# A four-layer mixer in f32r on one core: order of weight loads, of the first stores, and of the last tiles of an out-projection

## The chip, the core and the metric

The kernel runs on one core of one Trainium2 chip. Its time is the device time of one execution in microseconds (us); lower is better. Engines are named as in the profile: PE is TensorE's matmuls (PEld its weight loads), DVE is VectorE, ACT is ScalarE, POOL is GpSimd, SP is SyncE, which here issues nearly all DMAs from one queue that runs in order.

## The reference, cut to what matters

The input x has 2048 rows (tokens) of 1024 values in float32. Four layers follow each other. Each has one projection in, a mixer of its own, one projection out, a residual and (except the last) a layer norm:

```python
def reference(x, ...):
    x = first_block(x, ...)      # layer 1
    x = second_block(x, ...)     # layers 2 and 3
    return third_block(x, ...)   # layer 4

# the frame of every layer
h = jnp.einsum('btd,de->bte', x, w_in)        # 1024 -> 2560 to 4360 columns
mix = mixer(h)                                 # see below, 1024 columns
out = jnp.einsum('bte,ed->btd', mix, w_out)    # 1024 -> 1024
z = ALPHA * x + out                            # layer 4: x + out, and no norm behind it
x = (z - mu) * lax.rsqrt(var + LN_EPS) * ln_g + ln_b
```

The mixers are: layer 1, a gated linear recurrence in chunks and sliding-window attention with sinks; layer 2, gated linear attention and a spatial gating unit; layer 3, retention and multi-scale pooling; layer 4, banded attention, an mLSTM and a gated convolution, with an RMS norm of the input ahead. None of the mixers is touched by the change.

## The kernel before

**Blocks.** The 2048 tokens are four blocks of 512, each of four tiles of 128. `run` (the end of the class) goes through the blocks in pairs: layer 1 on blocks 0 and 1, layer 2 on blocks 0 and 1, layers 3 and 4 likewise, then all four layers on blocks 2 and 3. That makes sixteen pairs of layer and block.

**Split operands.** A float32 product is made of three f32r matmuls: each operand is split into a rounded part (`hi`, for the input `ah`) and the rest (`lo`, `al`), and hi x hi, hi x lo and lo x hi are added up in PSUM.

**Weights.** Weights come in pieces of 128 x 1024 (some 128 x 528 or 128 x 544), by `weight` (L441). The first time that a piece is used (layer and block 0) it is loaded unsplit into a staging tile `wst` (two buffers), cast by ACT into `hi` (L450), and DVE subtracts to get `lo` (L315, the helper of every two-tensor operation). The split piece, tile `whl` (four buffers, 1 MB each), is then stored to DRAM (tile `wdr`, L454). In the other three blocks the piece is ready: one DMA brings it back (L446). A projection in has 20 to 36 pieces, a projection out eight. The first projection of a block, `in_b4`, holds four pieces at a time and does the first 256 tokens with each of them, then the other 256: eight groups of 24 matmuls.

**Who sets the order.** Every instruction is written once in program order; a scheduler then sets each engine's fixed order at build time, by priority and by its own estimate of times. `hp()` makes what is written inside it count as 2500 instructions earlier, `later(n)` as n instructions later; `keep_in_program_order` keeps the marked instructions in the order in which they are written. `weight` is all inside `hp()`, and at the start (`self.start`) its loads and those of the input are kept in program order by `first`.

**The start.** `load_x` (L521 and on) loads the first block's input in eight tiles of 256 KB (tile `u`, L545), two at a time, each two followed by one of the first four weight pieces. ACT casts the input into `ah` (L548), DVE subtracts into `al` (L315).

**The projection out** (`out_proj`). The output has two halves of 512 columns. The first half takes four pieces, and for each the four tiles of tokens in turn, in four PSUM banks (`acc`). The second half takes pieces 4 to 7 all at once and goes tile by tile: all eight chunks of tile 0, then tile 1, and so on, 24 matmuls a tile, and behind each tile its residual (L312), statistics (L628), the reciprocal root by nine small DVE operations (`rstd1`: tiles `ve`, `vy`, `vh`, `vf`, `vt`) and the norm. Even tiles are normed by ACT (`nm`, `vy`) without gain and bias; odd ones by four DVE operations. What is left of a tile (`tail`: eight transposes on PE, `mm<-ident,big`, their copies and stores, and for even tiles four POOL operations on the tile) is put off, and `flush` writes it between the groups of the next block's `in_b4`. Layer 4 has no norm and no tail: its tiles are stored (`out_dram`, L625).

Of the kernel before, what the change touches and what calls it, by code (L numbers as in the profile page):

```python
# [10 lines left out]
F32 = mybir.dt.float32  # L11
# [5 lines left out]
ALU = mybir.AluOpType  # L17
# [209 lines left out]
class Build:  # L227
    def __init__(self, ctx, tc, I, O, layers=(1, 2, 3, 4), nblk=NB):
        self.tc, self.nc, self.I, self.O = tc, tc.nc, I, O
        self.layers, self.nblk = layers, nblk  # L230
        pool = lambda name, bufs, **k: ctx.enter_context(tc.tile_pool(name=name, bufs=bufs, **k))
        self.c1 = pool("c1", 1)
        self.wst = pool("wst", 2)
        self.whl = pool("whl", 4)
        self.up = pool("up", 13)
        self.tp = pool("tp", 7)
        self.sp = pool("sp", 4)
        self.lp = pool("lp", 1)
        self.bp = pool("bp", 1)
        self.dp = pool("dp", 1, space=bass.MemoryType.DRAM)  # L240
        self.wdr = pool("wdr", 1, space=bass.MemoryType.DRAM)
        self.parts = {}
        self.ps_a = pool("ps_a", 4, space=PSUM)
        self.ps_m = pool("ps_m", 4, space=PSUM)

# [193 lines left out]
    def weight(self, name, i, n=1024):  # L439
        nc = self.nc  # L440
        with self.hp():  # L441
            w = self.whl.tile([128, 2, n], F32R, tag="whl", name="whl")
            hi, lo = w[:, 0], w[:, 1]
            kept = self.parts.get((name, i))
            if kept is not None:
                nc.sync.dma_start(w.bitcast(F32), kept)  # L446
                return hi, lo
            st = self.wst.tile([128, n], F32, tag="wst", name="wst")
            self.first(nc.sync.dma_start(st, self.I[name][i][:, 0:n]))
            nc.scalar.copy(hi, st)  # L450
            self.tt(lo, st, hi.bitcast(F32), ALU.subtract)
            if self.nblk > 1:
                kept = self.wdr.tile([128, 2, n], F32, tag=f"{name}_{i}", name="wdr")
                nc.sync.dma_start(kept, w.bitcast(F32))  # L454
                self.parts[name, i] = kept
        return hi, lo

    def next_w(self, n=1024):
        if self.ahead:
# [61 lines left out]
    def load_x(self, b, l):  # L521
        if not self.start:
            for t in range(4):
                for i in range(2):
                    self.load_x1(b, l, t, i)
            return

        ws = []
        self.wi, self.wpos = "wi1", 0
        for parts in (((0, 0), (1, 0)), ((0, 1), (1, 1)), ((2, 0), (3, 0)), ((2, 1), (3, 1))):  # L530
            for t, i in parts:
                with self.hp():
                    self.load_x1(b, l, t, i)
            ws.append(self.next_w())
        self.ahead, self.start = ws, False

    def first(self, ins):
        if self.start:
# [36 lines left out]
    def out_proj(self, layer, b, split):  # L575
# [35 lines left out]
        for j in range(4):  # L611
            hi, lo = self.weight(wo, 4 + j)
            ws.append((hi.rearrange("p (k c) -> p k c", k=2), lo.rearrange("p (k c) -> p k c", k=2)))
            if j == 0:
                for i in range(2):
                    for t in range(0):
                        self.out_mm(acc[t], t, i, ws[0][0][:, i], ws[0][1][:, i])
        for t in range(4):
            for k in range(2 if t < 0 else 0, 8):
                hi, lo = ws[k // 2]  # L620
                self.out_mm(acc[t], t, k, hi[:, k % 2], lo[:, k % 2])
            x = self.xr[:, t, 512:1024]
            self.stt(x, x, alpha, acc[t], ALU.mult, ALU.add)
            if layer == 4:
                nc.sync.dma_start(self.O[b * TB + t * 128:b * TB + t * 128 + 128, :], self.xr[:, t])  # L625
                continue
            st = sts[t]
            nc.vector.bn_stats(st[:, 6:12], x)  # L628
            x = self.xr[:, t]
            mv = self.s(2, "mv")  # L630
            nc.vector.bn_aggr(mv, st)
            y = self.rstd1(mv[:, 1:2], 1.0, 1e-5)
            if not last and t % 2 == 0:
                nm = self.s(1, "nm")
                self.stt(nm, mv[:, 0:1], -1.0, y, ALU.mult, ALU.mult)
                self.act(x, x, AF.Identity, scale=y, bias=nm)
                continue
            for i in range(2):
                xi = x[:, i * 512:i * 512 + 512]
                self.stt(xi, xi, mv[:, 0:1], lng[i], ALU.subtract, ALU.mult)  # L640
                self.stt(xi, xi, y, lnb[i], ALU.mult, ALU.add)
            if last:
                nc.sync.dma_start(self.O[b * TB + t * 128:b * TB + t * 128 + 128, :], x)
# [1111 lines left out]
    def run(self):  # L1755
        self.setup()

        self.todo = [(l, c) for b in range(0, self.nblk, 2) for l in self.layers for c in range(b, b + 2)]
        self.lc = None
        while self.todo:  # L1760
            l, c = self.todo.pop(0)
            self.load_x(c, l)
# [36 lines left out]
```

## Time and profile before

| | |
|---|---|
| median of three runs | 3770.92 us (3770.17 to 3778.2) |
| the profiled execution's own time | 3774.09 us |
| its span, first to last instruction | 3772.3 us |
| PE busy | 3677.3 us (97%) |
| DVE, ACT, POOL busy | 2177.9, 1384.2, 542.1 us |
| DMA | 798.04 MB, 212 GB/s over the span |
| mean granted clock of PE | 0.995 |

Busy times are shares of the span; PE's matmuls are pipelined and their ends are modelled, so that a busy PE need not be a PE at its peak. A wait is put down to what ended it. The granted clock is the share of full speed that the throttle left to PE.

### The profile page before, as it was taken

The numbers are of one execution on the slowest core, as the hardware profiler recorded it, in microseconds if no ns is written. First come the engines' busy times: TensorE is split into PE (matmuls) and PEld (weight loads), VectorE is DVE, ScalarE is ACT, GpSimd is POOL, SyncE is SP. The second block draws the span as 40 slices with busy tenths as digits, with TensorE's granted clock in tenths as the row PEclk, the third lists the DMA queues.
The fourth block names the chain that finished last, engine by engine and source line by source line (L and its number), as shares of the span: only waits on it lengthen the run. The fifth ranks groups of instructions, "written<-read, shape, count | busy, mean of one in ns | idle before, by whom it ended". The sixth has DMA issues, their size and how long they took to land.

```text
span 3772.3 us, 53592 instructions
## 1 busy us (share of the span) xinstructions
PE 3677.3 (97%) x20576; PEld 3100.4 (82%) x20576; DVE 2177.9 (58%) x5387; ACT 1384.2 (37%) x2889; POOL 542.1 (14%) x445
## 2 busy tenths in 40 slices
PE   7999999999999999999999999999999999999999
PEld 6788888887888888788888878888887878888887
DVE  6765556555655598577456455443544545872873
ACT  5636343323241354325254263312221313441441
POOL 0020111112121200300200201111121311011002
PEclk9999999999999999999999999999999999999999
DMA  6775567855886576752544645747565756435434
GB/s 229 261 263 177 187 239 273 311 199 195 300 304 215 213 260 223 261 197 101 208 179 164 226 152 187 255 161 256 185 231 206 253 193 246 146 140 209 177 123 157
DMA packets 161680, 798.04 MB, mean 212 GB/s; under 512 B 17936, under 2 KB 18064, under 8 KB 93840
## 3 DMA queue, kind: packets, MB, share of 16 engines
q1 hardware_dynamic: 161424, 794.62, 58.4%
q8 instruction: 162, 2.65, 0.3%
q14 instruction: 94, 0.77, 0.1%
HBM read 593.02 MB, written 201.52 MB: 211 GB/s over the span
## 4 chain that ended last, share of the span: by engine, by line
PE 49%; DVE 6%; DMA 2%; ACT 2%; issue 1%; POOL 0%; SPq 0%; DVEq 0%; POOLq 0%; ACTq 0%
PE acc L324 41%; PE mm L324 6%; PE mm L327 3%; DVE u L312 2%; DMA whl<-wdr 1%; DVE t L315 1%; ACT t L301 0%; DVE big L312 0%; DMA wst<-in_wo_dram 0%; DVE t L1034 0%; DVE ss L1400 0%; ACT u L301 0%; POOL mix L315 0%; DVE mix L312 0%; ACT u L1424 0%
## 5 line engine op out<-in xcount | busy, mean ns | idle before, releaser
L324 PE MATMUL acc<-whl,ah 128*128 128x512 f32 (+3 forms) x6144 | 1816.2, 380 | 15.1 <-DVE whl L315 4.1
L324 PEld LDWEIGHTS acc<-whl,ah 128*128 128x128 f32 x6144 | 1112.0, 188 | 242.9 <-issue 7.1
L324 PE MATMUL acc<-whl,al 128*128 128x512 f32 (+3 forms) x3072 | 1156.8, 377 | 0.0
L324 PE MATMUL acc<-ah,whl 128*128 128x256 f32 (+1 forms) x4096 | 1076.8, 346 | 46.0 <-DVE whl L315 17.3
L324 PEld LDWEIGHTS acc<-ah,whl 128*128 128x128 f32 x4096 | 707.1, 191 | 135.0 <-DVE whl L315 18.6
L324 PE MATMUL acc<-al,whl 128*128 128x512 f32 (+1 forms) x2048 | 699.2, 342 | 0.5 <-DVE al L315 0.2
L324 PEld LDWEIGHTS acc<-whl,al 128*128 128x128 f32 x3072 | 578.0, 188 | 114.0
L324 PEld LDWEIGHTS acc<-al,whl 128*128 128x128 f32 x2048 | 391.5, 191 | 40.5 <-issue 2.9
L315 DVE TENSOR_TENSOR whl<-wst,whl 128x1024 fp32r<-128x1024 f32 (+2 forms) x140 | 173.3, 1244 | 142.0 <-ACT whl L450 131.5
L315 POOL TENSOR_TENSOR big<-big,u 128x512 f32<-128x512 f32 x96 | 139.1, 1471 | 562.0 <-PE mm L327 421.6
L450 ACT CAST whl<-wst 128x1024 fp32r<-128x1024 f32 (+2 forms) x140 | 143.3, 1027 | 149.3 <-DMA wst<-in_wi_dram 76.1
L548 ACT CAST ah<-u 128x512 fp32r<-128x512 f32 x128 | 79.3, 619 | 307.0 <-PE acc L324 200.1
L312 DVE SCALAR_TENSOR_TENSOR g<-g,acc 128x512 f32<-128x512 f32 x80 | 54.6, 686 | 204.3 <-ACT g L301 204.2
L312 DVE SCALAR_TENSOR_TENSOR u<-mix,hdw,u 128x512 f32<-128x512 f32 x240 | 165.6, 742 | 0.1
L315 POOL TENSOR_TENSOR mix<-mix,g 128x512 f32<-128x512 f32 x56 | 77.4, 1385 | 592.2 <-DVE g L312 574.2
L312 DVE SCALAR_TENSOR_TENSOR big<-big,acc 128x512 f32<-128x512 f32 x128 | 86.7, 684 | 120.2 <-PE acc L324 118.5
L301 ACT ACTIVATE g<-acc 128x512 f32<-128x512 f32 x72 | 42.6, 596 | 232.0 <-PE acc L324 226.4
L301 ACT ACTIVATE t<-mm,cols 128x128 f32<-128x128 f32 (+2 forms) x272 | 99.6, 463 | 66.6 <-PE mm L327 62.7
L315 POOL TENSOR_TENSOR u<-u,lc 128x512 f32<-128x512 f32 (+1 forms) x64 | 68.0, 1070 | 326.1 <-issue 170.0
L315 DVE TENSOR_TENSOR al<-u,ah 128x512 fp32r<-128x512 f32 x128 | 89.7, 702 | 42.1 <-ACT ah L548 41.0
L324 PE MATMUL mm<-big,u 128*128 128x256 f32 (+2 forms) x616 | 94.3, 289 | 7.3 <-ACT big L923 1.8
L324 PEld LDWEIGHTS mm<-big,u 128*128 128x128 f32 x616 | 84.3, 191 | 16.0 <-ACT u L1424 3.2
(342 smaller groups left out, 4376.8 us busy)
## 6 DMA issues: line engine op xcount, KB each, us to landing
whl<-wdr SPq DMA_DIRECT2D x396, 1024.0 KB, 4.8
wdr<-whl SPq DMA_DIRECT2D x132, 1024.0 KB, 5.3
wst<-in_wi_dram SPq DMA_DIRECT2D x100, 512.0 KB, 6.9
rows<-big SPq DMA_DIRECT2D x48, 512.0 KB, 4.0
chn<-t SPq DMA_DIRECT2D x96, 256.0 KB, 6.3
u<-chn SPq DMA_DIRECT2D x96, 256.0 KB, 6.6
big<-rows SPq DMA_DIRECT2D x48, 512.0 KB, 7.1
wst<-in_wo_dram SPq DMA_DIRECT2D x32, 512.0 KB, 6.0
```

What stands on the lines that cost most here:

```text
L301: return self.nc.scalar.activation(out, in_, f, bias=bias, scale=scale)
L312: return self.nc.vector.scalar_tensor_tensor(out, in0, s, in1, op0, op1)
L315: return (eng or self.nc.vector).tensor_tensor(out, a, b, op)
L324: return self.nc.tensor.matmul(out, lhsT, rhs, start=start, stop=stop)
L327: return self.nc.tensor.transpose(out, in_, self.ident)
L450: nc.scalar.copy(hi, st)
L548: nc.scalar.copy(h, c4(st))
```

## The change

Three things change. (1) `weight` knows the order of all pieces (`pieces`), and when it is asked for a ready piece and one of the next two in that order is unsplit, it first writes that piece's load into `wst` (`stage`), ahead of the ready piece's load. (2) At the start, the very first piece is loaded, cast and subtracted in two halves; the four first pieces' stores are collected in `unsaved` and written behind all input loads and the layer's constants (`lc`), with a lower priority. (3) In the second half of a projection out, tiles 0 and 1 are accumulated together, chunk by chunk, and then tiles 2 and 3. Lines that did nothing before (`range(0)`, `t < 0`) go.

```diff
@@ -239,7 +239,7 @@
         self.bp = pool("bp", 1)
         self.dp = pool("dp", 1, space=bass.MemoryType.DRAM)
         self.wdr = pool("wdr", 1, space=bass.MemoryType.DRAM)
-        self.parts = {}
+        self.parts, self.staged, self.unsaved = {}, {}, []
         self.ps_a = pool("ps_a", 4, space=PSUM)
         self.ps_m = pool("ps_m", 4, space=PSUM)
 
@@ -441,19 +441,55 @@
         with self.hp():
             w = self.whl.tile([128, 2, n], F32R, tag="whl", name="whl")
             hi, lo = w[:, 0], w[:, 1]
+
+            assert self.order.pop(0) == (name, i, n)
+            if not self.start:
+                for a, k, m in self.order[0:2]:
+                    if (a, k) not in self.parts and (a, k) not in self.staged and (name, i) in self.parts:
+                        self.staged[a, k] = self.stage(a, k, m)
             kept = self.parts.get((name, i))
             if kept is not None:
                 nc.sync.dma_start(w.bitcast(F32), kept)
                 return hi, lo
-            st = self.wst.tile([128, n], F32, tag="wst", name="wst")
-            self.first(nc.sync.dma_start(st, self.I[name][i][:, 0:n]))
-            nc.scalar.copy(hi, st)
-            self.tt(lo, st, hi.bitcast(F32), ALU.subtract)
+            st = self.staged.pop((name, i), None) or self.stage(name, i, n)
+            parts = 2 if self.start and i == 0 else 1
+            for p in range(parts):
+                c = slice(p * n // parts, (p + 1) * n // parts)
+                nc.scalar.copy(hi[:, c], st[:, c])
+                self.tt(lo[:, c], st[:, c], hi[:, c].bitcast(F32), ALU.subtract)
             if self.nblk > 1:
                 kept = self.wdr.tile([128, 2, n], F32, tag=f"{name}_{i}", name="wdr")
-                nc.sync.dma_start(kept, w.bitcast(F32))
                 self.parts[name, i] = kept
+                self.unsaved.append((kept, w))
+                if not self.start:
+                    self.save()
         return hi, lo
+
+    def stage(self, name, i, n):
+        st = self.wst.tile([128, n], F32, tag="wst", name="wst")
+        parts = 2 if self.start and i == 0 else 1
+        for p in range(parts):
+            c = slice(p * n // parts, (p + 1) * n // parts)
+            self.first(self.nc.sync.dma_start(st[:, c], self.I[name][i][:, c]))
+        return st
+
+    def save(self):
+        while self.unsaved:
+            kept, w = self.unsaved.pop(0)
+            self.nc.sync.dma_start(kept, w.bitcast(F32))
+
+    def pieces(self):
+
+        for l, c in list(self.todo):
+            i = 0
+            for mode, cols in plan(l):
+                n = len(cols)
+                per = chunks_per_tile(n)
+                for _ in range(8 // per):
+                    yield f"wi{l}", i, per * n
+                    i += 1
+            for i in range(8):
+                yield f"wo{l}", i, 1024
 
     def next_w(self, n=1024):
         if self.ahead:
@@ -533,6 +569,9 @@
                     self.load_x1(b, l, t, i)
             ws.append(self.next_w())
         self.ahead, self.start = ws, False
+        self.lc = self.lconst(l, b)
+        with self.later(300):
+            self.save()
 
     def first(self, ins):
         if self.start:
@@ -611,14 +650,13 @@
         for j in range(4):
             hi, lo = self.weight(wo, 4 + j)
             ws.append((hi.rearrange("p (k c) -> p k c", k=2), lo.rearrange("p (k c) -> p k c", k=2)))
-            if j == 0:
-                for i in range(2):
-                    for t in range(0):
-                        self.out_mm(acc[t], t, i, ws[0][0][:, i], ws[0][1][:, i])
-        for t in range(4):
-            for k in range(2 if t < 0 else 0, 8):
-                hi, lo = ws[k // 2]
-                self.out_mm(acc[t], t, k, hi[:, k % 2], lo[:, k % 2])
+        for t in range(4):
+
+            if t % 2 == 0:
+                for k in range(8):
+                    hi, lo = ws[k // 2]
+                    for t1 in (t, t + 1):
+                        self.out_mm(acc[t1], t1, k, hi[:, k % 2], lo[:, k % 2])
             x = self.xr[:, t, 512:1024]
             self.stt(x, x, alpha, acc[t], ALU.mult, ALU.add)
             if layer == 4:
@@ -1757,6 +1795,7 @@
 
         self.todo = [(l, c) for b in range(0, self.nblk, 2) for l in self.layers for c in range(b, b + 2)]
         self.lc = None
+        self.order = list(self.pieces())
         while self.todo:
             l, c = self.todo.pop(0)
             self.load_x(c, l)
```

## The prediction

> **What bounds the kernel now.** I read the page first, then the waits of TensorE (PE), then busy times by stage.
>
> ```profile
> span 3772.3 us, 53592 instructions
> PE 3677.3 (97%) x20576; PEld 3100.4 (82%) x20576; DVE 2177.9 (58%) x5387; ACT 1384.2 (37%) x2889; POOL 542.1 (14%) x445
> ```
>
> PE is busy for 3677.3 of 3772.3 us, and the change removes no matmul. So it can only win back idle time, some 95 us, and time in which PE ran at a lower clock. The waits of PE name the idle time (total, times, longest):
>
> ```profile
> PE acc L324 <- DVE whl L315: 21.4, 8, 6.1
> PE acc L324 <- ACT whl L450: 10.8, 3, 10.0
> PE acc L324 <- ACT ah L548: 9.7, 3, 4.3
> PE acc L324 <- DMA whl<-wdr: 7.8, 9, 2.0
> ```
>
> The first three are waits for pieces being split and for input being split; the fourth is for ready pieces. All sit at the starts of blocks. The busy time by stage shows what they cost with the clock (columns: stretch, length, PE busy and matmuls, the same for weight loads, DVE, ACT and POOL, then granted clock, DMA share, GB/s):
>
> ```profile
> 10.00:49.41 39.41, 28.76 (x194) 27.06 (x195) 16.36 (x29) 12.30 (x19) 0.29 (x1) 0.96 0.67 237
> 512.75:530.15 17.40, 11.62 (x77) 11.21 (x76) 9.54 (x9) 4.97 (x11) 6.70 (x7) 0.80 0.60 221
> 932.86:950.11 17.25, 11.47 (x77) 11.07 (x76) 9.55 (x9) 5.08 (x11) 6.24 (x6) 0.80 0.60 210
> 1299.44:1316.61 17.17, 11.10 (x74) 10.90 (x75) 8.61 (x7) 5.50 (x16) 5.89 (x5) 0.80 0.59 218
> 1602.47:1625.11 22.64, 22.64 (x194) 22.64 (x195) 1.38 (x2) 0.63 (x1) 0.47 (x1) 1.00 0.58 202
> 1905.23:1929.62 24.39, 24.39 (x194) 24.39 (x195) 7.58 (x16) 5.43 (x11) 0.29 (x1) 0.93 0.64 233
> ```
>
> The undisturbed row is 1602: a whole first projection in 22.64 us, 0.117 us a matmul. The kernel's start (row 1) takes 39.41 for the same, 16.8 us more, after 10.0 us in which PE has nothing. The three rows with x77, x77 and x74 are the starts of layers 2, 3 and 4 in their first block, where weights are unsplit; at 0.117 they would take 9.0, 9.0 and 8.7, so they lose 8.4, 8.2 and 8.5: 25 us.
>
> **The change, part by part.**
>
> *Start: stores behind the inputs, first piece in halves.* The timeline of the start (start, length, engine, line, tile; in brackets the idle time before and what ended it):
>
> ```profile
> 8.90 1.04 ACT L450 CAST whl<-wst 128x1024 fp32r<-128x1024 f32 x1 [2.17 <-DMA wst<-in_wi_dram]
> 10.00 0.58 PE L324 MATMUL acc<-ah,whl 128*128 128x256 f32 x1 [10.00 <-ACT whl L450]
> 11.23 0.33 SPq L454 DMA_DIRECT2D wdr<-whl  x1
> 11.60 1.41 SPq L545 DMA_DIRECT2D u<-in_xt_dram  x2
> 13.06 0.98 SPq L449 DMA_DIRECT2D wst<-in_wi_dram  x1
> 16.79 1.27 ACT L548 CAST ah<-u 128x512 fp32r<-128x512 f32 x2 [6.73 <-DMA u<-in_xt_dram]
> 21.01 0.33 SPq L454 DMA_DIRECT2D wdr<-whl  x1
> ```
>
> SP's queue runs in order and the input loads are held in program order, so the store of piece 0 waits on SP until VectorE (DVE) has split the piece at 11.2, and the loads behind it wait too: SP issues nothing from 3.1 to 11.2. Then 1 MB of store runs ahead of 0.5 MB of input and 0.5 MB of weights, and input is cast only at 16.79. The same turn repeats every 9.8 us (11.23, 21.01, ...). With the stores behind, loads follow at some 0.45 us per issue. Half of piece 0 (256 KB) should be there 1.1 us earlier at the 237 GB/s of row 1, and its cast takes half of 1.04, so PE begins near 8.3. In all 4 MB must come, 17 us at that rate. Two staging buffers let piece 2 load only when piece 0 is split (about 10) and piece 3 when piece 1 is (about 14), so piece 3 is usable near 22 to 26, with one store possibly slipped ahead. PE has three quarters of its 22.64 us to do before it needs piece 3. So the projection ends between 33 (everything filled in, 8.3 + 22.64 and 2 for a cold clock) and 41 (late loads, order kept), against 49.4: I take 36, a gain of 13, between 8 and 17. The four delayed stores hold their buffers longer; later pieces have slack of several us, and that is in the pass-on below.
>
> *Staging ahead of ready pieces.* It acts only where the current piece is ready and one of the next two is not: six loads, at the starts of layers 2, 3 and 4. The trace before already has them early:
>
> ```profile
> 238.45 0.44 SPq L449 DMA_DIRECT2D wst<-in_wi_dram  x1
> 244.05 0.42 SPq L449 DMA_DIRECT2D wst<-in_wi_dram  x1
> 503.28 1.66 SPq L454 DMA_DIRECT2D wdr<-whl  x2
> 504.99 2.29 SPq L449 DMA_DIRECT2D wst<-in_wi_dram  x2
> 508.14 10.85 POOL L315 TENSOR_TENSOR big<-big,u 128x512 f32<-128x512 f32 x8 [47.18 <-DVE nm L312]
> 509.97 0.14 DVE L320 TENSOR_SCALAR vh<-ve 128x1 f32<-128x1 f32 x1
> 514.12 1.20 DVE L312 SCALAR_TENSOR_TENSOR vt<-vy,vf 128x1 f32<-128x1 f32 x1
> 517.82 2.38 DVE L312 SCALAR_TENSOR_TENSOR big<-big,vy,u 128x512 f32<-128x512 f32 x2
> 520.12 2.35 DVE L315 TENSOR_TENSOR whl<-wst,whl 128x1024 fp32r<-128x1024 f32 x2
> 521.39 0.80 PE L324 MATMUL acc<-ah,whl 128*128 128x256 f32 x2 [5.57 <-DVE whl L315]
> ```
>
> The two loads at 238 and 244 are layer 2's pieces 0 and 1: the scheduler's priority already lifts them as soon as both staging buffers are free, 260 us before use. I cost this part at 0. PE waits here for pieces 2 and 3: their loads leave at 504.99 because their staging buffers come free only when pieces 0 and 1 are split, and these wait for a `whl` buffer of the out-projection.
>
> *Out-projections two tiles at a time.* The second half is 96 matmuls at 0.234 us, by the chain's last row:
>
> ```profile
> 3754.98 13.08 PE acc L324 x56
> 1596.20 4.52 SPq L446 DMA_DIRECT2D whl<-wdr  x4
> 1602.47 0.36 PE L324 MATMUL acc<-ah,whl 128*128 128x256 f32 x1 [1.21 <-DMA whl<-wdr]
> 1905.23 0.36 PE L324 MATMUL acc<-ah,whl 128*128 128x256 f32 x1 [2.00 <-DMA whl<-wdr]
> ```
>
> Before, its four pieces are last used after 78, 84, 90 and 96 matmuls; now after 60, 72, 84 and 96. Piece 0's buffer is free 18 x 0.234 = 4.2 us earlier, the next two 2.8 and 1.4. For ready pieces the load that left at 1596.20 leaves near 1592, so the first-piece waits (7.8 us in all, 2.0 the longest) go; so does the cold clock after the longest (24.39 - 22.64 = 1.75). Gain 9.5; I would keep 6 of it at the least. For unsplit pieces the same 4.2 us bring pieces 0 and 1 forward to about 498 and 501, and the loads of 2 and 3 by 3 to 6 us.
>
> What is late next there is DVE. The split of piece 2 was queued behind the layer norm of the last tile, and that ran slowly: from 508.14 to 518.99 GpSimd (POOL) runs eight operations on the finished tiles, and in that time DVE's operations with two SBUF inputs take 1.20 us on one column where the one-input one takes 0.14. Now tiles 2 and 3 end together, so tile 2's norm falls after the end as well. Its price, from the start of layer 1's second block, where POOL was still idle for tile 2:
>
> ```profile
> 259.18 0.68 DVE L312 SCALAR_TENSOR_TENSOR big<-big,acc 128x512 f32<-128x512 f32 x1
> 263.49 0.16 DVE L312 SCALAR_TENSOR_TENSOR nm<-mv,vy 128x1 f32<-128x1 f32 x1
> 263.69 1.24 ACT L301 ACTIVATE big<-big,nm,vy 128x1024 f32<-128x1024 f32 x1 [2.36 <-DVE nm L312]
> 263.54 1.91 PE L327 MATMUL mm<-ident,big 128*128 128x128 f32 x16
> 269.44 0.49 PE L327 MATMUL mm<-ident,big 128*128 128x128 f32 x3
> ```
>
> Tile 2's chain takes 4.5 us (259.18 to 263.65) with no POOL beside it. In that trace it is over as the out-projection ends (263.70); after the change it begins there. With its first piece in time PE does group 0 (24 x 0.117 = 2.8 us), then tile 0's eight transposes (half of 1.91), so POOL starts some 3.8 us after the end. By then DVE has done the additions and statistics of both tiles; the six two-input operations left in tile 2's chain then meet four POOL operations of 1.36 us (10.85 / 8), and the chain is over near 9.4. With the scaling on ACT (1.24) tile 2 is ready at 10.6; its transposes are due after three groups and two tiles' transposes, 10.4. That is a wait of 0 to 1.7; I take 0.5 at nine boundaries, -4.5. At the three unsplit starts the split of piece 3 sits in the same queue; I leave 2.0 us of wait and 0.7 of clock each, so 25 becomes a gain of 17, between 5 (piece 3 as late as now) and 25.
>
> The Trainium skill states this lock as a rule: SBUF — State Buffer, section "Who interferes with whom", has a DVE instruction with two SBUF inputs fully blocked by a GpSimd instruction that reads SBUF. It speaks against ending two tiles at once; the trace agrees (1.20 against 0.16 us for one column of two inputs), and the slow rival below is what it would do at its worst.
>
> A second rule bears on the clock: TensorE: Matmul & The Clock Gate, "Part 1", lets the clock drop after about 3.4 us idle. By that alone my 2.0 us of remaining wait would leave the clock whole and the 17 would be 19; the row at 1905, a 2.00 us gap followed by a clock of 0.93, disagrees, so I keep the 0.7.
>
> *The end.* Now two tiles' last additions and stores follow the last matmul.
>
> ```profile
> 3768.08 0.69 DVE L312 SCALAR_TENSOR_TENSOR big<-big,acc 128x512 f32<-128x512 f32 x1 [4.91 <-PE acc L324]
> out_dram<-big SPq DMA_DIRECT2D x2, 512.0 KB, 2.6
> ```
>
> That is one more 0.69, and two stores share the engines: +0.7 to +2.0, I take 1.2.
>
> *Pass-on.* With PE 6 to 13 us earlier in the blocks that split weights, later pieces come relatively later; DMA is busy to 0.6 to 0.7 there, so most of the slack holds. I take -2, between 0 and -6. The new order of the matmuls itself I cost at nothing: the first half of every out-projection interleaves four tiles already.
>
> *Sum*: 13 + 17 + 9.5 - 4.5 - 1.2 - 2 = 31.8 us. The profiled execution took 3774.09 us (1.8 more than its span) and would take 3742; the median is 3.2 lower, so 3739.
>
> **The rivals.**
>
> *The lock eats the transitions.* If DVE's queue keeps the splits of pieces 2 and 3 behind both norm chains, the three starts stay as long as now, and tile 2 waits 1.0 us at nine places: 13 + 0 + 9.5 - 9 - 1.2 - 2 = 10, 3761. For it: the split at 520.12 stands right behind the chain. Against: the scheduler orders by its own times, in which pieces 2 and 3 now come 3 to 6 us earlier.
>
> *Slower: the transposes of tile 2 wait.* PE's order is fixed at build time. In the trace they stand 5.7 us after the end (269.44). If they stay there and tile 0's transposes stay right at the end (263.54), POOL begins at once, the six two-input steps cost 1.2 each instead of 0.2 (+6), and with tile 3's first two operations (+1.3) tile 2's chain is over 11.8 us after the end and its scaling on ACT near 13. PE waits 5 us or more at twelve boundaries, 60 us or more less what the gains return (36 without that term): 24 slower, 3795; it decides for slower from 3 us a boundary. Against: both positions came about because the first pieces were late, and they no longer are.
>
> *Staging does act*, and the unsplit starts lose nothing: 25 instead of 17, 3731. Against it stand the loads at 238 and 244.
>
> *No change*: gains at the start pass on into a wait for stores and the rest cancels; 3771. Against: the start's 16.8 us are a queue's order, not a bound.
>
> **How the numbers follow.** Forecast 0.67 (3739, its own range 3720 to 3753), lock eats the transitions 0.14 (3761), staging acts 0.05 (3731), slower 0.07 (3795), no change 0.07. About 0.2%, 7.5 us, is what a measurement of this kernel can tell from no change. Faster 0.67 + 0.13 + 0.05 = 0.85, same 0.01 + 0.07 = 0.08, slower 0.07. The upper ends of the gains together (17 + 25 + 9.5 - 1) give 3720; the lower ends reach past no change, so the range goes to 3764, which takes in the lock and leaves out the last two cases and a little on the fast side.
>
> **What would show it.** Right: SP issues the input loads with at most one store of weights among them; PE starts near 8 us and the first 192 matmuls end near 36; the x77 stages shrink to 10 to 13 us with the clock at 1.00; the wait of PE for `whl<-wdr` falls below 2 us in all. The two staged loads of layer 2 stay near 238 and 244. Wrong: `mm<-ident,big` appears among PE's waits with over 20 us, DVE's norm chain fills the stretch after each out-projection, or PE waits for the split of pieces at 520 as long as now.

## The result and the profile after

The changed kernel took 3736.39 us (median of 4 runs, 3735.43 to 3739.72) against 3773.11 us for the kernel before (4 runs, 3770.17 to 3778.2) on the same chip: a ratio of 0.9903, 95% interval 0.9886 to 0.992. The forecast was 3739. The profiled execution took 3735.56 us, 1.8 more than its span.

The page's first lines of the changed kernel:

```profile
span 3733.8 us, 53637 instructions
PE 3662.3 (98%) x20576; PEld 3091.1 (83%) x20576; DVE 2208.4 (59%) x5388; ACT 1384.6 (37%) x2890; POOL 538.0 (14%) x445
```

The span is 38.5 us shorter. PE's busy time fell by 15 us with the same number of matmuls, while its mean granted clock rose from 0.995 to 0.998: some 11 of the 15 us (0.003 of the span) were matmuls at a lower clock. The other 23.5 us are idle time. What is left of that stands in the waits of PE (total, times, longest):

```profile
PE acc L324 <- ACT whl L458: 6.9, 1, 6.9
PE mm L327 <- ACT t L301: 6.3, 9, 0.7
PE acc L324 <- DMA whl<-wdr: 5.7, 4, 2.0
PE mm L324 <- DVE u L312: 5.3, 10, 1.2
PE mm L327 <- ACT big L301: 5.1, 3, 2.2
```

The 21.4 us for `DVE whl` and the 9.7 for `ACT ah` are off the top. New are the second row, nine waits of up to 0.7 us at transposes, and the last, three waits for the scaling of tile 2. The third row has its old name but another place, as will be seen. Two smaller rows grew as well, inside the mixers of layers 3 and 4: `DVE nq L315` from 2.0 to 4.5 us and `DVE big L312` from nothing to 4.1. The changed kernel without GpSimd's work, further down, has them too (4.1 and 3.8 us), so they aren't its doing; what causes them is open.

The start, from the timeline (the cast and the first matmul, the third piece's load and the first store), and then as a stage:

```profile
6.27 0.62 ACT L458 CAST whl<-wst 128x512 fp32r<-128x512 f32 x1
6.94 0.58 PE L324 MATMUL acc<-ah,whl 128*128 128x256 f32 x1 [6.94 <-ACT whl L458]
9.20 0.33 SPq L473 DMA_DIRECT2D wst<-in_wi_dram  x1
16.63 0.43 SPq L479 DMA_DIRECT2D wdr<-whl  x1
```

```profile
6.94:32.93 25.99, 25.67 (x194) 24.87 (x195) 16.97 (x31) 13.55 (x21) 0.29 (x1) 1.00 0.96 366
```

Loads stand ahead of the first store, which leaves at 16.63 and not at 11.23. The first projection ends at 32.93 in place of 49.41, and while it runs the DMA engines move 366 GB/s, not 237. This trace is one of the better ones: in the ten traces of kernels that have this start (the first piece in halves, the stores behind) the projection ends between 32.63 and 35.52, at 327 to 377 GB/s.

The three starts with unsplit weights, from the first transpose of a finished tile to the last: the first three rows are the kernel before, the next three the changed one. Both hold the same matmuls (a record can be missing).

```profile
507.40:530.75 23.35, 17.57 (x130) 17.16 (x129) 14.76 (x21) 10.19 (x23) 11.31 (x9) 0.85 0.70 254
927.51:950.71 23.20, 17.42 (x130) 17.02 (x129) 14.76 (x21) 10.30 (x23) 10.85 (x8) 0.85 0.70 243
1293.77:1317.21 23.44, 17.29 (x129) 16.85 (x128) 14.21 (x15) 10.88 (x28) 10.82 (x8) 0.85 0.68 246
```

```profile
491.51:508.81 17.30, 15.06 (x130) 14.62 (x128) 16.48 (x31) 9.75 (x22) 11.61 (x10) 1.00 0.80 294
906.71:923.98 17.27, 15.03 (x130) 14.62 (x129) 16.45 (x31) 9.71 (x22) 11.05 (x8) 1.00 0.82 287
1273.85:1290.68 16.83, 15.48 (x130) 14.66 (x129) 16.48 (x30) 10.94 (x29) 11.19 (x8) 1.00 0.76 278
```

They shrink from 69.99 to 51.40 us in sum, 18.6 us, and the clock in them rises from 0.85 to 1.00. The parts of some 77 matmuls that the prediction priced take 11.04, 11.00 and 10.55 us, at a clock of 1.00. GpSimd is as busy as before (the fifth of the busy times), and VectorE is busy nearly all the time.

### The profile page after: what moved, and what is told of

Its sections match the earlier page's. It is cut to its first block, busy times and chain, and to the rows that moved or that the text cites. A ratio compares the mean times of both kernels' runs of the same rounds, so it can differ in the third digit from the quotient of the medians.

```text
span 3733.8 us, 53637 instructions
## 1 busy us (share of the span) xinstructions
PE 3662.3 (98%) x20576; PEld 3091.1 (83%) x20576; DVE 2208.4 (59%) x5388; ACT 1384.6 (37%) x2890; POOL 538.0 (14%) x445
## 4 chain that ended last, share of the span: by engine, by line
PE 80%; DVE 11%; ACT 4%; DMA 2%; issue 2%; POOL 1%; SPq 0%; ACTq 0%; DVEq 0%; POOLq 0%
PE acc L324 67%; PE mm L324 9%; PE mm L327 4%; DVE u L312 2%; DMA wst<-in_wi_dram 1%; DVE whl L315 1%; DMA whl<-wdr 1%; DVE t L315 1%; DVE vt L312 1%; ACT t L301 1%; DVE big L312 1%; DVE vy L312 1%; DVE al L315 0%; ACT big L301 0%; ACT whl L458 0%
## 5 line engine op out<-in xcount | busy, mean ns | idle before, releaser
L324 PE MATMUL acc<-ah,whl 128*128 128x256 f32 (+1 forms) x4096 | 1064.8, 344 | 9.3 <-ACT whl L458 6.9
L324 PEld LDWEIGHTS acc<-ah,whl 128*128 128x128 f32 x4096 | 699.6, 189 | 94.3 <-issue 7.5
L315 DVE TENSOR_TENSOR whl<-wst,whl 128x1024 fp32r<-128x1024 f32 (+3 forms) x141 | 176.5, 1254 | 122.2 <-ACT whl L458 115.6
L315 POOL TENSOR_TENSOR big<-big,u 128x512 f32<-128x512 f32 x96 | 129.6, 1377 | 595.2 <-DVE vf L320 374.9
L458 ACT CAST whl<-wst 128x1024 fp32r<-128x1024 f32 (+3 forms) x141 | 143.5, 1020 | 193.5 <-PE acc L324 100.6
L312 DVE SCALAR_TENSOR_TENSOR g<-g,acc 128x512 f32<-128x512 f32 x80 | 54.6, 686 | 205.4 <-ACT g L301 205.3
L312 DVE SCALAR_TENSOR_TENSOR big<-big,acc 128x512 f32<-128x512 f32 x128 | 86.4, 680 | 140.8 <-PE acc L324 140.5
L312 DVE SCALAR_TENSOR_TENSOR u<-mix,hdw,u 128x512 f32<-128x512 f32 x240 | 165.7, 744 | 0.1
L315 POOL TENSOR_TENSOR mix<-mix,g 128x512 f32<-128x512 f32 x56 | 78.6, 1408 | 592.1 <-DVE g L312 574.4
L315 DVE TENSOR_TENSOR al<-u,ah 128x512 fp32r<-128x512 f32 x128 | 87.3, 690 | 55.0 <-ACT ah L587 43.3
L315 POOL TENSOR_TENSOR u<-u,lc 128x512 f32<-128x512 f32 (+1 forms) x64 | 67.1, 1056 | 319.9 <-issue 236.8
```

The source lines that it names most:

```text
L312: return self.nc.vector.scalar_tensor_tensor(out, in0, s, in1, op0, op1)
L315: return (eng or self.nc.vector).tensor_tensor(out, a, b, op)
L324: return self.nc.tensor.matmul(out, lhsT, rhs, start=start, stop=stop)
L458: nc.scalar.copy(hi[:, c], st[:, c])
```

## The experiments

The theory after the result: the start's gain is a matter of the order in SP's queue; the pairs gain because the first pieces' buffers come free earlier; and what is still lost after each out-projection is VectorE's norm chain, held up by GpSimd. The rivals stand in the expectations. Every ratio is against the kernel before on the same chip, in runs beside it.

### The change in its parts

**The start alone**: the changed kernel with the loads ahead and the pairs taken out.

```diff
-            if not self.start:
-                for a, k, m in self.order[0:2]:
...
-                        self.staged[a, k] = self.stage(a, k, m)
...
-            if t % 2 == 0:
-                for k in range(8):
-                    hi, lo = ws[k // 2]
-                    for t1 in (t, t + 1):
-                        self.out_mm(acc[t1], t1, k, hi[:, k % 2], lo[:, k % 2])
+            for k in range(8):
+                hi, lo = ws[k // 2]
+                self.out_mm(acc[t], t, k, hi[:, k % 2], lo[:, k % 2])
```

> The changed start alone (inputs ahead of the stores, first piece in halves); out-projections one tile at a time as before, no staging. Theory: the start is worth what the trace after shows there, 16.5 us (first 192 matmuls end at 32.93 against 49.41), and all of it reaches the end, because no later wait of PE hangs on the stores: 3755 to 3758 us, 0.9954 to 0.9962 of before, and the three starts with unsplit weights still take some 17 us for 77 matmuls. Rival (pass-on): with PE 16 us earlier in the first blocks, pieces that have to be loaded and split come later for PE, and a third or more of the gain is given back by the end of layer 4's first pair: 3761 to 3765 us.

Measured: 3755.84 us against 3769.43, ratio 0.9963 (0.995 to 0.9976), 13.6 us less. The trace tells the two theories apart better than the time. VectorE's last addition of an out-projection, in layer 1's first block and in layer 4's second, first in the kernel before and then here:

```profile
263.74 0.69 DVE L312 SCALAR_TENSOR_TENSOR big<-big,acc 128x512 f32<-128x512 f32 x1
1903.27 0.69 DVE L312 SCALAR_TENSOR_TENSOR big<-big,acc 128x512 f32<-128x512 f32 x1 [1.69 <-PE acc L324]
```

```profile
249.06 0.69 DVE L312 SCALAR_TENSOR_TENSOR big<-big,acc 128x512 f32<-128x512 f32 x1
1891.32 0.69 DVE L312 SCALAR_TENSOR_TENSOR big<-big,acc 128x512 f32<-128x512 f32 x1 [1.69 <-PE acc L324]
```

The first projection ends 14.1 us earlier than in the kernel before (35.32 against 49.41). The lead is 14.7 us after the first block and 12.0 after eight: most of the gain arrives, and some 2.7 us are given back. In the three unsplit starts little has changed: 23.22, 22.26 and 22.95 us for the same stages, at a clock of 0.85.

**The pairs alone**: the kernel before with only the loop over pairs (the same lines the other way round).

> The kernel before with the second half of each out-projection two tiles at a time and nothing else. Theory: the pairs alone bring what is left of the difference, 19 to 24 us (36.7 less 16.5, and a little for what the two share): 3749 to 3754 us, with the three starts with unsplit weights at 10 to 13 us for 77 matmuls at full clock and the waits for a first ready piece gone. Rival: the unsplit starts gain because the new start leaves the queue of stores and the staging buffers in another state, not because of the pairs: then they stay near 17 us here and the time is 3760 or more.

Measured: 3751.61 against 3769.43, ratio 0.9953 (0.9938 to 0.9968), 17.8 us less, a little under the 19 to 24 expected and far from the rival's 3760. The stages in this kernel:

```profile
506.66:524.18 17.52, 15.05 (x130) 14.62 (x128) 16.70 (x31) 9.72 (x22) 11.79 (x10) 1.00 0.81 298
921.90:940.51 18.61, 16.39 (x130) 16.19 (x129) 16.46 (x31) 9.57 (x22) 11.04 (x8) 0.91 0.81 291
1290.16:1307.43 17.27, 15.43 (x129) 14.60 (x128) 16.92 (x32) 10.92 (x29) 11.63 (x8) 1.00 0.75 274
```

The unsplit starts shrink by the pairs, whatever the start does; the clock of 0.91 in the second row follows a wait of 2.22 us for tile 2's scaling. The waits for the first ready pieces are gone here too, and three waits for the fifth piece (4.1 us in all) stand in their place. The two parts together make 31.4 us of the 36.7. Their intervals (9 to 19 us for the start, 12 to 23 for the pairs) hold the missing 5, so these times don't show that the parts help each other.

**The first piece whole**: in `weight` and in `stage`

```diff
-            parts = 2 if self.start and i == 0 else 1
+            parts = 1
```

> The changed kernel with its first piece loaded and split whole, not in halves. Theory: PE begins near 8.9 us in place of 6.94 and the first 192 matmuls end 1 to 2 us later, so the time is 1 to 2 us over the changed kernel's, 3737 to 3739. Rival: PE has to wait for the third and fourth piece anyway, the halves only move the idle time about, and the time is the changed kernel's within 0.5 us.

Measured: 3735.19 against 3769.43, ratio 0.9907 (0.9892 to 0.9922), the same as the changed kernel's 0.9903. PE begins at 9.44 instead of 6.94. The first projection ends at 35.39, which lies within the 32.63 to 35.52 of the ten traces with halves, so even at that point no gain shows, and by the end of the kernel the times can't be told apart. The theory's 1 to 2 us are neither shown nor excluded.

**No loads ahead**:

```diff
-                for a, k, m in self.order[0:2]:
+                for a, k, m in self.order[0:0]:
```

> The changed kernel without the loads ahead of ready pieces (the loop over the next two pieces runs over none). Theory: 0, because the order of the loads is the same as with it: the two loads of layer 2's first pieces stay near 222 and 228 us, as in the changed kernel, and the time is the changed kernel's within 0.1%, 3733 to 3740 us. Rival: the loop is what brings the loads early and the three unsplit starts lose 5 us each without it: near 3750 us.

Measured: 3735.61, ratio 0.9904 (0.9887 to 0.9921). Without the loop every engine gets the same instructions in the same order as with it, so the loop over the next pieces does nothing in this kernel. As the same program, its trace also shows what differs from one execution to the next: PE waits 2.1 us for ready pieces in place of 5.7, and the first projection ends at 34.18 in place of 32.93. In the changed kernel the two early loads (a view of their line: count, durations, first and last start) still stand long before the end of layer 1's second block:

```profile
L473 SPq DMA_DIRECT2D wst<-in_wi_dram x2: 423/428/432, 221.3 to 226.9; - x2
```

### What holds VectorE

After an out-projection of the changed kernel (layer 1's first block), VectorE's, ScalarE's, GpSimd's and PE's rows from the timeline:

```profile
249.90 0.22 DVE L312 SCALAR_TENSOR_TENSOR vt<-vy,vh 128x1 f32<-128x1 f32 x1
249.97 5.05 POOL L315 TENSOR_TENSOR big<-big,u 128x512 f32<-128x512 f32 x4 [47.18 <-DVE vf L320]
250.15 1.15 DVE L312 SCALAR_TENSOR_TENSOR vy<-vt,vy 128x1 f32<-128x1 f32 x1
251.34 1.22 DVE L312 SCALAR_TENSOR_TENSOR vt<-vy,vf 128x1 f32<-128x1 f32 x1
252.59 1.21 DVE L312 SCALAR_TENSOR_TENSOR vt<-vt 128x1 f32<-128x1 f32 x1
253.84 1.21 DVE L312 SCALAR_TENSOR_TENSOR vy<-vt,vy 128x1 f32<-128x1 f32 x1
255.07 0.16 DVE L312 SCALAR_TENSOR_TENSOR nm<-mv,vy 128x1 f32<-128x1 f32 x1
255.27 1.25 ACT L301 ACTIVATE big<-big,nm,vy 128x1024 f32<-128x1024 f32 x1 [3.88 <-DVE nm L312]
256.42 1.49 ACT L301 ACTIVATE t<-mm,cols 128x128 f32<-128x128 f32 x4
257.96 0.66 PE L327 MATMUL mm<-ident,big 128*128 128x128 f32 x4 [0.73 <-ACT t L301]
```

GpSimd's four operations on tile 0 last from 249.97 to 255.02. Four of VectorE's one-column steps with two SBUF inputs lie in that stretch and take 1.15 to 1.22 us each; the one before it took 0.22 and the one behind it 0.16. So these six steps of tile 2's chain take 5.3 us; at 0.16 to 0.22 us each they would take about 1. ScalarE's queue is in order: the scaling of tile 2 stands ahead of the second half of tile 0's evictions, so these start only at 256.42, the transposes' PSUM buffers stay full, and PE waits 0.73 us at 257.96. That is the row with the nine waits. At the three unsplit starts it is the scaling itself that PE waits for (5.1 us).

**GpSimd's work on the rows left out**, in the kernel before and in the changed one:

```diff
-        if t % 2 == 0:
-            for i in range(2):
-                xi = x[:, i * 512:i * 512 + 512]
-                self.tt(xi, xi, lng[i], ALU.mult, nc.gpsimd)
-                self.tt(xi, xi, lnb[i], ALU.add, nc.gpsimd)
```

> The kernel before without GpSimd's work after an out-projection: the multiplication by the norm's gain and the addition of its bias on tiles 0 and 2 of the rows are left out (the activations that go on by the transposed way keep theirs). Theory: at the three starts with unsplit weights the split of piece 2 is late because VectorE's chain for the last tile is locked by GpSimd; without it the two-input steps on one column take 0.16 to 0.25 us, the chain is over some 6 us earlier and the waits of 5.57, 5.23 and 6.07 us shrink to under 1 each with the clock whole: 15 to 20 us faster, 3749 to 3755. Rival: the load of pieces 2 and 3, which leaves only when a staging buffer is free, sets the wait: then it stays at 4 us or more and the time is within 6 us of before.

Measured: 3740.94 against 3769.91, ratio 0.9918 (0.9899 to 0.9936), 29.0 us less, more than the 15 to 20 expected. The three stages:

```profile
506.86:522.04 15.18, 14.97 (x130) 14.74 (x128) 7.09 (x21) 10.20 (x23) 0.83 (x2) 1.00 0.92 325
921.82:937.32 15.50, 14.96 (x129) 14.74 (x128) 7.09 (x21) 10.30 (x23) 0.00 (x0) 1.00 0.90 325
1280.02:1294.97 14.95, 14.87 (x130) 14.63 (x128) 6.35 (x15) 10.89 (x28) 0.00 (x0) 1.00 0.93 333
```

VectorE has the same 21 and 15 instructions as in the kernel before and needs 7.09 and 6.35 us for them in place of 14.76 and 14.21. The stages take 45.63 us, 24.4 less, with one-tile out-projections and late loads (those of pieces 2 and 3 leave at 504.45, in the kernel before at 504.99). The shortest that any run shows for these stages is 44.0 us, so nearly all of the loss at the unsplit starts was the lock; the rival (the loads leave late) falls.

> The changed kernel without the same work of GpSimd (gain and bias on the rows of tiles 0 and 2 left out); the order of the instructions of TensorE is unchanged. Theory: the waits of PE for the scaling of tile 2 (5.1 us at three starts) and for the evictions that stand behind it in ScalarE's queue (6.3 us at nine) both come from VectorE's locked chain; they vanish, and the time is 9 to 12 us below the changed kernel's: 3724 to 3727. Rival: the waits come from the number of VectorE's steps after the end of two tiles at once (18 steps and six wide ones), not from the lock: at most 3 us are gained, 3733 or more.

Measured: 3712.76, ratio 0.9843 (0.9822 to 0.9864), 23.6 us below the changed kernel's median (22.6 by the two ratios) and twice what was expected. Both waits are gone, and so are the 5.7 us for ready pieces, which nobody had put down to GpSimd. The stages fall to 14.7 us each, 44.0 in sum. The difference between the two runs without GpSimd, 28.2 us, is what start and pairs bring when there is no lock.

### Moving GpSimd's work

**Tile 0's operations behind tile 2's** (GpSimd's instructions are held in this order):

```diff
-        if t % 2 == 0:
-            for i in range(2):
-                xi = x[:, i * 512:i * 512 + 512]
...
-        nc.sync.dma_start(self.rows[layer, b % 2][t], x)
+        for t1 in {0: (), 1: (1,), 2: (2, 0), 3: (3,)}[t]:
+            x = xr[:, t1]
+            if t1 % 2 == 0:
...
+                    self.tc.keep_in_program_order(self.tt(xi, xi, lng[i], ALU.mult, nc.gpsimd))
...
+            nc.sync.dma_start(self.rows[layer, b % 2][t1], x)
```

> The changed kernel with GpSimd's work on tile 0 moved behind that on tile 2, nothing left out; on GpSimd it then starts after tile 2's transposes. Theory (lock): tile 2's chain runs unlocked and tile 2 is ready near 6 us after the end, so the waits for it and behind it go (11.4 us); GpSimd's eight operations now meet tile 3's chain and the splits that stand behind it, which costs up to 3 us back at the three unsplit starts: 3725 to 3731. Rival (number of steps): no gain, 3733 to 3738. A third way: the later rows keep their buffers and stores longer and the next block's reload waits: slower than the changed kernel.

Measured: 3749.5 against 3769.91, ratio 0.9941 (0.9922 to 0.9961): 13 us slower than the changed kernel. What the theory says of the lock came: both waits behind tile 2's chain are gone and the three stages take 44.0 us. But the third way came on top of it and outweighs it. The row of PE's waits for ready pieces, and then GpSimd, SP and PE around one boundary:

```profile
PE acc L324 <- DMA whl<-wdr: 17.3, 9, 3.4
```

```profile
259.21 10.85 POOL L315 TENSOR_TENSOR big<-big,u 128x512 f32<-128x512 f32 x8 [54.55 <-PE mm L327]
264.93 0.38 SPq L708 DMA_DIRECT2D chn<-t  x1
270.09 0.32 SPq L716 DMA_DIRECT2D rows<-big  x1
270.50 1.31 SPq L452 DMA_DIRECT2D whl<-wdr  x1
277.72 0.47 PE L324 MATMUL acc<-ah,whl 128*128 128x512 f32 x1 [2.82 <-DMA whl<-wdr]
```

The store of tile 0's rows waits in SP's queue until GpSimd has ended at 270.06; the load of the fifth ready piece stands right behind it and leaves at 270.50. That is 20.2 us after VectorE's last addition; the same load leaves after 17.4 us in the changed kernel and after 14.9 without GpSimd's work. The queue was blocked at its head. The 17.3 us are 11.6 more than in the changed kernel and not the whole loss: four other new or longer waits, of 1.7 to 2.7 us each, stand behind VectorE's later work.

**The rows of tiles 0 and 2 stored from GpSimd's queue**, with this order and with that of the changed kernel:

```diff
-        nc.sync.dma_start(self.rows[layer, b % 2][t], x)
+        (nc.sync if t % 2 else nc.gpsimd).dma_start(self.rows[layer, b % 2][t], x)
```

> GpSimd's work on tile 0 behind that on tile 2, as in the run with the late work, and those tiles' stores of rows on GpSimd's queue. Theory (head of the line): the 17.3 us that TensorE waited for ready pieces there came from loads queued behind stores that waited for the late GpSimd; they go, and what is left is the gain of the unlocked chain: 3722 to 3730. Rival (bandwidth or the lock in its new place): still 3740 or more.

Measured: 3736.06 against 3767.29, ratio 0.9917 (0.9898 to 0.9937). PE waits nowhere for a ready piece: the 17.3 us were the queue's head. The unlocked chain's gain is there at the three starts (44.0 us again), but not in the time, and neither of the two forecasts came. PE has new waits 31 to 39 us into a block, of 6.4 us (layer 1's fourth block), 3.9 (layer 2's first) and 3.8 (layer 3's first, in the second row); their cause is open:

```profile
PE mm L327 <- ACT t L870: 6.4, 1, 6.4
PE acc L324 <- DVE whl L315: 5.1, 3, 3.8
PE mm L327 <- DVE lrt L1141: 3.9, 1, 3.9
```

> The changed kernel with the stores of the finished rows of tiles 0 and 2 issued from GpSimd's queue in place of SyncE's; nothing else. Theory (head of the line): the loads of the fifth piece wait in SyncE's queue behind the store of tile 2's rows, which waits for GpSimd; with the store on another queue they leave 1 to 3 us earlier, and the waits of TensorE for that piece (5.7 us in four) fall under 2: 3730 to 3733, 3 to 6 us under the changed kernel. Rival (bandwidth): those loads are slow because some 3 MB of stores share the engines with them; then the waits stay and the time is the changed kernel's within 2 us.

Measured: 3735.43 against 3767.29, ratio 0.9913 (0.9897 to 0.9929), the changed kernel's time. The waits for ready pieces are 4.7 us in place of 5.7, which decides nothing, since two executions of the changed program itself show 5.7 and 2.1. The theory's first step didn't come: at the boundary shown above the load leaves 17.0 us after VectorE's last addition in place of 17.4, because SP's queue now stops for the store of another tile, 39.3 us in all for VectorE's last steps on tile 1 or 3 (`SPq L714 <- DVE big`). So the theory falls in this form, but the rival isn't shown by it.

### The norm without GpSimd

**All four tiles' norms on VectorE**, as tiles 1 and 3 have it:

```diff
-            if not last and t % 2 == 0:
+            if not last and t < 0:
...
-            if t % 2 and layer < 3:
+            if t >= 0 and layer < 3:
...
-                    if t % 2:
+                    if t >= 0:
...
-        if t % 2 == 0:
+        if t < 0:
```

> The changed kernel with the norm of tiles 0 and 2 done wholly on VectorE, as that of tiles 1 and 3 is: GpSimd's eight operations, ScalarE's scaling of the tile and the scaled evictions go, VectorE gets four wide operations more for each of the two tiles (2.9 us a tile). Theory (lock): the chains run unlocked, both waits behind them go (11.4 us) and with GpSimd out of the stores' way those for the fifth piece too (5.7): 3715 to 3723. Rival (number of steps): VectorE's queue gets 5.8 us longer at each boundary, tile 2 is ready no earlier than now and the splits at the unsplit starts come later: 3737 or more.

Measured: 3715.23 against 3767.29, ratio 0.9859 (0.984 to 0.9877), 21 us below the changed kernel (17 by the two ratios). The norm's one-column steps by their shapes (busy, mean ns), in the changed kernel and here:

```profile
L312 DVE SCALAR_TENSOR_TENSOR vy<-vt,vy 128x1 f32<-128x1 f32 x96 | 45.8, 477 | 2.7
L312 DVE SCALAR_TENSOR_TENSOR vt<-vy,vf 128x1 f32<-128x1 f32 x48 | 32.8, 682 | 1.3
```

```profile
L312 DVE SCALAR_TENSOR_TENSOR vy<-vt,vy 128x1 f32<-128x1 f32 x96 | 14.8, 154 | 0.5
L312 DVE SCALAR_TENSOR_TENSOR vt<-vy,vf 128x1 f32<-128x1 f32 x48 | 10.0, 209 | 0.4
```

And the page's line of this kernel:

```profile
PE 3659.2 (99%) x20576; PEld 3091.0 (83%) x20576; DVE 2158.6 (58%) x5460; ACT 1323.8 (36%) x2770; POOL 406.8 (11%) x349
```

VectorE has 72 instructions more and is busy 50 us less: what was taken off it was waiting, which counts as busy. The rival (the number of steps) falls. ScalarE has less to do here as well, but the changed kernel without GpSimd's work keeps all of ScalarE's and is as fast, so ScalarE isn't the cause. The waits for ready pieces, for tile 2's scaling and for the evictions behind it are all gone from PE's list, so the fifth piece's wait too came from GpSimd's work. The path begins in SP's queue: at the boundary shown above that load leaves 14.9 us after VectorE's last addition here and 17.4 in the changed kernel, right behind a store of rows and one of a transposed tile. Whether these stores also slow it on the DMA engines isn't shown.

**For tile 0 alone** (`t % 2 == 0` becomes `t == 2`, and its opposite `t != 2`):

> The same for tile 0 alone; tile 2 keeps GpSimd's four operations after its transposes. Theory (lock): tile 0's operations are what locks tile 2's chain, so the 11.4 us of waits for tile 2 go here as well; tile 3's chain still meets tile 2's operations and the store of tile 2's rows still stands ahead of the fifth piece: 3722 to 3728, above the run with both. Rival (number of steps): 3737 or more.

Measured: 3716.1, ratio 0.9861 (0.9845 to 0.9876), the same as with both and better than the 3722 to 3728 expected. Tile 0's operations did the damage; tile 2's do none that shows.

> The version with the norm of all tiles on VectorE once more, in more rounds, since it is the fastest and one of its four times was 4439.75 us. Theory: that time belongs to the execution, not to the kernel; 3713 to 3718 us, 0.984 to 0.988 of before, no such time again. Rival: something in the kernel (its order of stores and loads) can stall for hundreds of us; then a time over 4000 shows again.

Measured: 3712.31 us (five times, 3711.18 to 3717.67) against 3771.86, ratio 0.9842 (0.9829 to 0.9856). No such time came again; in that one execution the granted clock was 0.753, in the other three 0.998 to 1.000, and why it was low stays open. This version beats both kernels: its interval lies wholly below that of the changed kernel (0.9886 to 0.992).

## Why the prediction was right, point by point

- **What bounds it, and what is to be won.** Right: all of the gain is idle time and clock, as the page's first line shows. One reading was loose: of the 21.4 us of waits for VectorE's splits 4.1 lie 45 us and more into a block, not at its start.
- **Start, +13 (8 to 17).** The mechanism was right: SP issues all input loads ahead of the first store. This trace shows 16.5 us, near the upper end; the ten traces with this start show 13.9 to 16.8. The term mis-sized is the rate: 4 MB were taken at the 237 GB/s of the blocked start, a mean that takes in stretches such as that from 18 to 22 us, with 38 GB/s. The freed queue moves 327 to 377 GB/s, and in this trace PE waits at most 0.2 us for a piece once it has begun. PE began at 6.94, where 8.3 was forecast. The halves, which gave 1.7 us of that forecast, can't be seen in the time.
- **Pass-on, -2 (0 to -6).** With the start alone the lead shrank by 2.7 us over eight blocks.
- **Staging, 0.** Right, and for the reason given: the priority had lifted these loads already.
- **Three unsplit starts, +17 (5 to 25).** Measured 18.6 by stages, and 5.8 us are left against the stages of the kernel before without GpSimd (51.40 against 45.63), where the forecast left 8.1. What is left is the same lock, now on tile 2's chain. One of the signs that were listed for a wrong prediction came with it: VectorE's work fills these stretches (16.48 of 17.30 us in the first). The residual clock loss of 0.7 each didn't come. Two waits of 2.2 us there left the clock at 1.00, as the Trainium skill has it (TensorE: Matmul & The Clock Gate, "Part 1", a drop after about 3.4 us idle); but in the run with the pairs alone one such wait of 2.22 us stands in a stage at 0.91, so the rule is no guide to the single case.
  The step before it has to be corrected: the prediction let the loads of pieces 2 and 3 set the start and VectorE come next. The run of the kernel before without GpSimd shows that the loads cost next to nothing there (45.63 us for stages that take 44.0 in the changed kernel without GpSimd). What the pairs changed is the place of the splits in VectorE's queue: before, both stood behind the last tile's chain at 520.12. In the trace after, where their loads leave 5 to 9 us before the out-projection ends and not at its end, one stands ahead of tile 2's chain and the other inside it, ahead of its last two steps and of tile 3's chain:

```profile
490.88 1.21 DVE L315 TENSOR_TENSOR whl<-wst,whl 128x1024 fp32r<-128x1024 f32 x1
498.42 1.22 DVE L315 TENSOR_TENSOR whl<-wst,whl 128x1024 fp32r<-128x1024 f32 x1
```

- **First ready pieces, +9.5.** These waits and the cold clock behind them are gone. But 5.7 us appear at the fifth piece (2.1 in another execution of the same program), which the prediction didn't look at: it followed the first pieces' buffers and not what else is stored at the time when the next load leaves. The list of what would show it right had less than 2 us under this name; that item was wrong.
- **Tile 2's norm, -4.5 (0.5 at nine places).** Measured 6.3: 0.7 at eight of the nine places, nothing at the ninth, and 0.4 at an unsplit start. Right in size and cause; the path was one step longer (ScalarE's queue, and PSUM buffers that stay full), not the chain's own end.
- **The end, -1.2.** The last two additions of the kernel after:

```profile
3728.17 1.39 DVE L312 SCALAR_TENSOR_TENSOR big<-big,acc 128x512 f32<-128x512 f32 x2 [9.81 <-PE acc L324]
```

  They end at 3729.56, 4.2 us before the span does; in the kernel before the last one ends at 3768.77, 3.5 before. That is 0.7 us, the lower bound.
- **The sum.** 16.5 + 18.6 + 9.5 - 5.7 - 6.3 - 0.7 - 2.7 is 29.2; the profiled execution gained 38.5, the median 36.7. Of the missing 9.3 us 5.6 lie in one block that the prediction had no term for, layer 1's fourth block, first in the kernel before, then after:

```profile
2143.57:2391.07 247.50, 243.00 (x1350) 204.27 (x1349) 138.00 (x374) 114.38 (x276) 28.63 (x22) 0.99 0.53 187
```

```profile
2108.87:2350.76 241.89, 239.04 (x1350) 202.03 (x1350) 140.59 (x376) 114.13 (x276) 27.76 (x22) 1.00 0.53 191
```

  In the kernel before PE has four waits of 0.45 to 1.01 us between 2181.7 and 2186.0 there, 3.1 us in all, for operands that ScalarE (L923) and VectorE make in layer 1's mixer, and right behind them its granted clock is 0.50 from 2186 to 2190, and 0.83 in the mean over these 10 us:

```profile
2179.00:2189.00 10.00, 6.91 (x30) 5.55 (x29) 5.98 (x15) 6.07 (x12) 0.29 (x1) 0.83 0.51 184
```

  The changed kernel has none of these waits, and the start alone, with 242.90 us for this block, has 1.1 us of them. Why they go isn't known, and the last 3.7 us are not settled either. The start was taken too small by 1 to 4 us and one wait of up to 5.7 us was overlooked, and a gain of 5.6 us came that nobody had counted: that 3739 lies so near the 3736.39 is in part luck.
- **The slower rival** (tile 2's transposes wait 5 us at twelve places) had the right mechanism, and the waits were 0.7 and 2.2 us, below the 3 us from which it decides. The rule of the Trainium skill behind it (SBUF — State Buffer, "Who interferes with whom") agrees with the traces: a one-column step takes 477 ns on average in the changed kernel and 154 with GpSimd's work gone.

## What to carry to other kernels

Before an engine is blamed for being slow, look at what its same instruction takes when a neighbour is idle: here VectorE's busy time was partly a lock, and giving VectorE more work in place of GpSimd's made it less busy and the kernel some 20 us faster. When work is moved later, follow the store that waits for it and what stands behind that store in its queue. A load that must be early has no business behind a store that waits for an engine, at the start of the kernel as at each block.

## What the runs showed of the hardware that was not expected

- The DMA engines moved 366 GB/s (busy share 0.96) over 26 us at the start once no store stood ahead of the loads in SP's queue, against 237 GB/s at 0.67 before; ten traces of this start show 327 to 377.
- Time in which VectorE is locked counts as busy: 2208.4 us with 5388 instructions, and 2158.6 with 5460.
- An idle time of 2.2 us was followed by a stage at full clock twice and by one at 0.91 once (2.21, 2.21 and 2.22 us). Four waits of 0.45 to 1.01 us within 4.3 us were followed by a clock of 0.50.
